# Moving the prompt attention's steps ahead in a hand-written issue order, and its first row loads to another queue

## The chip, the cores and the metric

The kernel runs on one core of a Trainium2 chip. The metric is the device time of one execution in microseconds (us), the median of several runs. The engines are TensorE (PE, with its weight loads as PEld), VectorE (DVE), ScalarE (ACT), GpSimd (POOL) and SyncE (SP). Each engine works through its own instructions strictly in the order that was fixed at compile time. Transfers are issued from the queues of SP (`dma` in the code), ACT (`put`) and POOL (`later`).

## What is computed

One layer of a hybrid decoder, in f32, for 512 prompt tokens and 8 sampled tokens that share all weights. They are handled together as 520 columns:

```
x = x + 0.5 * swiglu_1(rmsnorm(x))
z = rmsnorm(x) @ w_in          # u | q | k | v | gate_a | gate_b
a = gelu(ssm(u) + D*u);  a = a * sigmoid(a @ w_glu)         # branch A, state-space
b = mix over 3 groups of dilated window attention(q, k, v)  # branch B
x = x + (sigmoid(gate_a) * (a @ w_proj_a) + sigmoid(gate_b) * (b @ w_proj_b)) @ w_out
x = x + 0.5 * swiglu_2(rmsnorm(x))
```

Outputs are the new rows, the states of the state-space branch and the key and value caches.

## The kernel before

A *product* is 128 output rows times 520 columns. Each f32 operand is split into two fp32r parts (`wh`+`wl`, `xh`+`xl`), and the helper `mm` (line 221) adds three partial products over the blocks of the inner dimension, so a product over 1024 rows is 8 blocks x 3 x 2 column halves = 48 matmuls. The weights come in one at a time: `wfetch` loads a tile `wr` on SP's queue (L175), ACT copies it to `wh` (L166) and DVE forms `wl` (L167); three weights are kept ahead. There are 212 weights, and the products keep their order on PE.

Between the two SwiGLUs the products follow as: two q/k blocks, eight u blocks, ten q/k blocks, six v blocks, sixteen gate blocks, eight `w_glu` blocks (called glu0 to glu7 here, and gate0 to gate15 before them), then the projections. The smaller work of the branches is written as Python generators. Each has a list of numbers, and `pace()`, called after a product, counts the products and advances a generator once for each number that is reached. The count is 19 after gate0, 34 after gate15, 35 after glu0. In this order at each count:

- `LV`: `leave` (L765), the state-space output: 8 steps of 48 small matmuls (L772 to L774), copies by ACT, and after every second step eight stores to `yD` on POOL's queue (L787). Its last steps stand at 27, 27, 28, 28.
- `NB`: `normal` (L902): `normalise` of q/k block 0 to 11 by DVE (L863), each fed by two broadcasts on POOL's queue (L857), the last two at 20; then `tokens(0)` at 24.
- `AT`: the attention, 19 steps. Steps 1 to 16 are `attention(r)` for four row blocks `r`; two steps make a *pair* (one `r`, two heads for each of two halves `hp`): scores on PE (L960), bias and maxima on DVE (L966, L972), exponentials on ACT (L975), transposes on PE (L980) and their copies on ACT (L981), the sum over values on PE (L989) and its copy on ACT (L991). The pairs are numbered 0 to 7 here. Step 17 is `exchange` (four transfers), 18 and 19 are `combine`.
- `KS` and `SM`: the attention of the sampled tokens over the caches (`scores`, L1075, and `samples`, L1085), from 29 and from 34.
- `YB`: `y_block` 0 to 7 (L1050), from 29 to 33: two loads of a block from `yD` on POOL's queue (L1053, L1054), a gelu in turns on ACT and DVE (L1056 to L1060), and the split into `yh` (ACT, L304) and `yl` (DVE, L305). The tiles of the gelu have two buffers each, so block m+2 is loaded when block m is split. `yh` and `yl` lie in memory that the state-space tiles free when the last store of `leave` has landed.

The product glu0 multiplies all eight pairs `yh`, `yl`. Two planes of PSUM (tag `sb`) hold the scores of one pair, and two tiles `p` its exponentials.

The instructions other than the products stand on each engine where a planner put them at compile time: among those that are ready in its own reckoning of time, the one written first goes first. So a number in `AT` sets from which product on a step may be placed, and before which other work it goes.

At the start, `FIRST` (L38) orders the first transfers: numbers below 8 are the blocks of x (L370), 8 to 11 the halves of the first two weights (`whalf`, L187), 12 is the third weight. From each block of x ACT makes `xh` (L257) and a square (L269), DVE makes `xl` (L258).

Of the kernel before, what the change touches and what calls it, by code (L numbers as in the profile page):

```python
# [44 lines left out]
SC = 1.9  # L45
LV = (21, 21, 22, 22, 27, 27, 28, 28)
NB = (15, 15, 16, 16, 17, 17, 18, 18, 19, 19, 20, 20, 24)
AT = (25, 26, 27, 28, 29, 30, 31, 32, 32, 33, 34, 34, 35, 35, 36, 36, 37, 38, 40)
KS = (29, 30, 30, 31, 31, 32, 32, 33)
SM = (34, 34, 37, 39, 40)  # L50
YB = (29, 29, 30, 30, 31, 31, 32, 33)
# [7 lines left out]
def build(tc, A):  # L59
    nc = tc.nc  # L60
    V, S, G, T = nc.vector, nc.scalar, nc.gpsimd, nc.tensor
    dma = nc.sync.dma_start
    put = nc.scalar.dma_start
# [105 lines left out]
    def wfetch():  # L169
        ap = next(stream, None)  # L170
        if ap is None:
            return
        n = ap.shape[1]
        raw = raws.next()
        dma(raw[:, 0:n], ap)  # L175
        h, l = whs.next(), wls.next()
        wsplit(raw[:, 0:n], h[:, 0:n], l[:, 0:n])
        ahead.append([(h[:, c:c + 512], l[:, c:c + 512]) for c in range(0, n, 512)])


    def whalf(i, c):
        if c == 0:
            start.append((next(stream), raws.next(), whs.next(), wls.next()))
            ahead.append([])
        ap, *tiles_ = start[i]
        raw, h, l = (t[:, c:c + 512] for t in tiles_)
        dma(raw, ap[:, c:c + 512])  # L187
        wsplit(raw, h, l)
        ahead[i].append((h, l))
# [177 lines left out]
    X = [pf.tile([128, NT], F32, name="x", tag="x", bufs=KB) for m in range(KB)]  # L367
    for step in FIRST:
        if step < KB:
            dma(X[step], A["xT"][step])  # L370
        elif step < 12:
            whalf(step % 2, (step - 8) // 2 * 512)
        else:
            wfetch()
# [783 lines left out]
    def outputs():  # L1158
        while len(ys) < KB:
            y_block(len(ys))  # L1160
            yield

    side.append((list(AT), attending))
    yout = outputs()
# [78 lines left out]
    X = []  # L1243
# [123 lines left out]
```

## Time and profile before

| | |
|---|---|
| median of 3 runs | 1280.14 us (1277.73 to 1282.16) |
| time of the profiled execution | 1280.84 us |
| span from its first to its last instruction | 1279.0 us |
| PE, PEld busy | 98%, 96% of the span |
| DVE, ACT, POOL busy | 56%, 34%, 13% |
| mean granted TensorE clock | 0.992 of full speed |
| moved | 188.7 MB read, 68.6 MB written |

The shares are of one profiled execution. Matmuls are pipelined and the ends of their rows are modelled, so that the count of matmuls in a stretch and its length say more than the busy time. The clock is one of two levels, 1.2 GHz (0.5 of full speed) and 2.4 GHz. A row "A <- B" says that A sat idle until B released it.

### The profile page before, as it was taken

The numbers are of one execution on the slowest core, as the hardware profiler recorded it, in microseconds if no ns is written. First come the engines' busy times: TensorE is split into PE (matmuls) and PEld (weight loads), VectorE is DVE, ScalarE is ACT, GpSimd is POOL, SyncE is SP. The second block draws the span as 40 slices with busy tenths as digits, with TensorE's granted clock in tenths as the row PEclk, the third lists the DMA queues.
The fourth block names the chain that finished last, engine by engine and source line by source line (L and its number), as shares of the span: only waits on it lengthen the run. The fifth ranks groups of instructions, "written<-read, shape, count | busy, mean of one in ns | idle before, by whom it ended". The sixth has DMA issues, their size and how long they took to land.

```text
span 1279.0 us, 25230 instructions
## 1 busy us (share of the span) xinstructions
PE 1258.8 (98%) x10575; PEld 1234.1 (96%) x10575; DVE 714.8 (56%) x1268; ACT 434.7 (34%) x695; POOL 161.0 (13%) x289
## 2 busy tenths in 40 slices
PE   8999999999999999998999999999999999999999
PEld 7999999999999999998999789999999999999998
DVE  6794455635555339988436768765544334434442
ACT  5332233222344233342344664433423122222320
POOL 0110010000103541004631210000000000000000
PEclk9999999999999999999999889999999999999999
DMA  6665364637566575237957725547545445433332
GB/s 223 222 214 175 93 239 159 182 100 239 186 188 203 131 174 160 91 104 225 258 163 231 261 77 153 164 161 231 203 171 186 133 148 198 129 103 108 115 104 88
DMA packets 94889, 214.00 MB, mean 167 GB/s; under 512 B 42052, under 2 KB 50528, under 8 KB 94008
## 3 DMA queue, kind: packets, MB, share of 16 engines
q1 hardware_dynamic: 61640, 136.32, 34.1%
q0 software_dynamic: 13680, 67.62, 15.7%
q10 hardware_dynamic: 19456, 8.46, 2.7%
q8 instruction: 83, 1.36, 0.4%
q14 instruction: 30, 0.25, 0.1%
HBM read 188.72 MB, written 68.60 MB: 201 GB/s over the span
## 4 chain that ended last, share of the span: by engine, by line
PE 91%; DMA 4%; issue 1%; SPq 1%; POOL 1%; ACT 1%; DVE 0%; ACTq 0%; POOLq 0%; DVEq 0%
PE bigB L221 44%; PE bigA L221 29%; PE third L221 13%; PE s L681 1%; DMA kvt<-qkD 1%; PE s L989 1%; DMA ut<-uD 1%; PE sb L960 1%; DMA vD<-tok 1%; DMA gD<-t_sq 0%; PE s L980 0%; DMA x<-in_xT 0%; DMA wr<-in_wg 0%; PE bigB L774 0%; DMA OB<-hD 0%
## 5 line engine op out<-in xcount | busy, mean ns | idle before, releaser
L166 ACT ACTIVATE wh<-wr 128x1024 fp32r<-128x1024 f32 (+3 forms) x212 | 214.3, 1011 | 599.7 <-PE bigB L221 245.0
L167 DVE TENSOR_TENSOR wl<-wr,wh 128x1024 fp32r<-128x1024 f32 (+3 forms) x212 | 246.1, 1161 | 66.0 <-ACT wh L166 64.7
L221 PE MATMUL bigB<-xh,wh 128*128 128x260 f32 (+1 forms) x1216 | 249.1, 286 | 0.3 <-ACT wh L166 0.3
L221 PE MATMUL bigB<-xl,wh 128*128 128x260 f32 (+1 forms) x1216 | 248.7, 284 | 0.0
L221 PE MATMUL bigB<-xh,wl 128*128 128x260 f32 (+1 forms) x1216 | 246.9, 284 | 0.0
L221 PEld LDWEIGHTS bigB<-xl,wh 128*128 128x128 f32 x1216 | 188.1, 188 | 2.4 <-issue 2.4
L221 PEld LDWEIGHTS bigB<-xh,wh 128*128 128x128 f32 x1216 | 187.6, 189 | 1.6 <-issue 0.5
L221 PEld LDWEIGHTS bigB<-xh,wl 128*128 128x128 f32 x1216 | 187.9, 188 | 0.9 <-issue 0.9
L221 PE MATMUL bigA<-xh,wh 128*128 128x260 f32 x704 | 143.3, 285 | 2.4 <-ACT xh L257 1.5
L221 PE MATMUL bigA<-xl,wh 128*128 128x260 f32 x704 | 142.4, 284 | 0.7 <-DVE xl L258 0.7
L221 PE MATMUL bigA<-xh,wl 128*128 128x260 f32 x704 | 142.1, 283 | 0.5 <-DVE wl L167 0.5
L120 POOL COPY pace<-ah 1x1 f32<-1x1 f32 x48 | 21.6, 449 | 750.2 <-ACT ah L301 750.2
L221 PEld LDWEIGHTS bigA<-xh,wh 128*128 128x128 f32 x704 | 109.0, 190 | 4.7 <-ACT xh L257 3.3
L221 PEld LDWEIGHTS bigA<-xl,wh 128*128 128x128 f32 x704 | 108.6, 189 | 1.4 <-DVE xl L258 1.4
L221 PEld LDWEIGHTS bigA<-xh,wl 128*128 128x128 f32 x704 | 108.9, 189 | 0.7 <-DVE wl L167 0.7
L221 PE MATMUL bigA<-ah,wh 128*128 128x260 f32 x352 | 71.2, 283 | 0.0
L221 PE MATMUL bigA<-al,wh 128*128 128x260 f32 x352 | 71.0, 283 | 0.0
L221 PE MATMUL bigA<-ah,wl 128*128 128x260 f32 x352 | 70.6, 282 | 0.0
L221 PE MATMUL third<-xh,wh 128*128 128x260 f32 x288 | 58.0, 282 | 0.0
L221 PE MATMUL third<-xh,wl 128*128 128x260 f32 x288 | 57.9, 283 | 0.0
L221 PE MATMUL third<-xl,wh 128*128 128x260 f32 x288 | 57.8, 282 | 0.0
L221 PEld LDWEIGHTS bigA<-ah,wh 128*128 128x128 f32 x352 | 54.2, 189 | 0.1
(386 smaller groups left out, 2071.2 us busy)
## 6 DMA issues: line engine op xcount, KB each, us to landing
out_okv<-in_kv POOLq DMA_DIRECT2D x32, 1023.5 KB, 6.4
wr<-in_wg SPq DMA_DIRECT2D x43, 512.0 KB, 3.6
wr<-in_wu SPq DMA_DIRECT2D x43, 512.0 KB, 3.6
wr<-in_win SPq DMA_DIRECT2D x42, 512.0 KB, 4.3
wr<-in_wd SPq DMA_DIRECT2D x32, 448.0 KB, 3.4
wr<-in_wd SPq DMA_DIRECT2D x16, 512.0 KB, 3.4
out_okv<-in_kv POOLq DMA_DIRECT2D x8, 1022.0 KB, 5.9
kvt<-in_kv SPq DMA_DIRECT2D x48, 128.0 KB, 4.5
```

Source lines behind the costliest of these rows:

```text
L120: ins = G.tensor_copy(pace[0:1, 0:1], t[0:1, 0:1])
L166: S.activation(h, raw, AF.Copy)
L167: V.tensor_tensor(l, raw, h, ALU.subtract)
L221: i = T.matmul(ps[:, hf, 0:x.shape[1]], lhsT=a[:, c], rhs=x, start=k == 0 and j == 0, stop=k == n - 1 and j == 2)
L681: mark(T.matmul(ps[:, ri], lhsT=mp[:, a * 2 + ri], rhs=ut[:, a, 8:CW], start=True, stop=True))
L960: T.matmul(o, lhsT=q[pr, qc], rhs=k[pr, kc], start=True, stop=True)
L989: T.matmul(po[x * 64:x * 64 + 64, l * 128:l * 128 + 128], lhsT=vt[:, kt, c:c + 64], rhs=pTs[x][:, j], start=j in (j0, 2), stop=j % 2 == 1)
```

## The change

The numbers of `AT` become smaller, so that the attention's pairs are written after gate4 to gate11 (the last one in two halves, at 30 and 31) instead of after gate6 to glu1; `exchange` goes from 37 to 32, the two halves of `combine` from 38 and 40 to 33 and 36. The eight blocks of x are loaded from ACT's queue instead of SP's.

```diff
-AT = (25, 26, 27, 28, 29, 30, 31, 32, 32, 33, 34, 34, 35, 35, 36, 36, 37, 38, 40)
+AT = (23, 23, 24, 24, 25, 25, 26, 26, 27, 27, 28, 28, 29, 29, 30, 31, 32, 33, 36)
...
     for step in FIRST:
         if step < KB:
-            dma(X[step], A["xT"][step])
+            put(X[step], A["xT"][step])
         elif step < 12:
             whalf(step % 2, (step - 8) // 2 * 512)
```

No other line changes.

## Rows read from the trace of the kernel before

**Rows 1.** Windows, line 221 alone: length, busy (matmuls), clock, DMA share, GB/s.

```profile
792.45:895.81 103.36, 103.36 (x867) 103.36 (x866) 1.00 0.57 186
682.30:691.80 9.50, 7.31 (x49) 6.04 (x48) 1.00 0.87 275
717.93:748.46 30.53, 8.77 (x49) 7.49 (x49) 0.72 0.39 126
```

**Rows 2.** Windows, whole: PE, PEld, DVE, ACT, POOL busy, clock, DMA share, GB/s.

```profile
0.00:28.85 28.85, 24.36 (x157) 19.71 (x157) 18.96 (x44) 16.76 (x25) 2.14 (x10) 0.94 0.71 229
7.30:10.70 3.40, 3.35 (x15) 2.75 (x14) 2.35 (x5) 2.81 (x5) 0.00 (x0) 0.50 0.91 252
727.50:744.60 17.10, 14.84 (x84) 11.43 (x83) 11.62 (x23) 9.96 (x28) 3.67 (x6) 0.50 0.12 32
```

**Rows 3.** PE's groups of the stretch 717.93:748.46: count, busy us, mean ns, idle before.

```profile
L989 PE MATMUL s<-pT,vt 128*64 128x128 f32 x48 | 6.6, 375 | 0.2 <-ACT pT L981 0.2
L960 PE MATMUL sb<-qk 64*128 64x128 f32 (+1 forms) x26 | 5.4, 376 | 0.0
L980 PE MATMUL s<-ident,p 128*128 128x128 f32 x24 | 4.8, 343 | 1.2 <-ACT p L975 1.2
```

**Rows 4.** Timeline of ACT and DVE: first and last split of the y blocks.

```profile
683.67 0.63 ACT L304 ACTIVATE yh<-t_G 128x520 fp32r<-128x520 f32 x1
...
745.66 0.68 DVE L305 SCALAR_TENSOR_TENSOR yl<-t_G,yh 128x520 fp32r<-128x520 f32 x1
```

**Rows 5.** Groups of 640:748.5, ACT's of the attention, DVE's of y.

```profile
L975 ACT ACTIVATE p<-p,own 128x256 f32<-128x256 f32 (+1 forms) x30 | 14.6, 488 | 7.1 <-DVE own L972 7.0
L981 ACT ACTIVATE pT<-s 128x512 f32<-128x512 f32 (+1 forms) x16 | 8.9, 568 | 13.1 <-PE s L980 8.6 <-DMA kvt<-qkD 4.6
...
L1060 DVE SCALAR_TENSOR_TENSOR t_G<-t_T,t_G 128x520 f32<-128x520 f32 x8 | 5.5, 693 | 0.3 <-ACT t_T L1059 0.2
```

**Rows 6.** Timeline: the last normalised block (DVE), pair 0's last scores (PE).

```profile
630.53 0.75 DVE L863 SCALAR_TENSOR_TENSOR qk<-OB,gains,qk 128x512 f32<-128x512 f32 x1
...
634.17 0.49 PE L960 MATMUL sb<-qk 64*128 64x128 f32 x4
```

**Rows 7.** Timeline of POOL: last stores of `leave`; loads of y blocks 3, 5, 7.

```profile
670.16 4.23 POOL L787 DMA_DIRECT2D yD<-XS  x8 [8.44 <-ACT XS L780]
...
686.76 0.75 POOL L1053 DMA_DIRECT2D t_G<-yD  x1
...
714.16 0.76 POOL L1053 DMA_DIRECT2D t_G<-yD  x1 [2.73 <-DVE yl L305]
...
730.38 0.75 POOL L1053 DMA_DIRECT2D t_G<-yD  x1 [0.42 <-DVE yl L305]
```

**Rows 8.** Tile `t_G`, 684:748: its loads, from issue to landing.

```profile
DMA to landing us min/median/max: 3.0/5.1/6.3
```

**Rows 9.** Timeline of ACT, 698:706: a store that ACT issues, and what follows it.

```profile
704.13 0.33 ACTq L887 DMA_DIRECT2D gD<-t_sq  x1
704.51 0.60 ACT L981 ACTIVATE pT<-s 128x512 f32<-128x512 f32 x1 [4.56 <-DMA kvt<-qkD]
```

**Rows 10.** Timeline of the start: ACT's first work, SP's third weight, PE's waits.

```profile
0.74 1.28 ACT L166 ACT_TABLE_LOAD   x1 [0.74 <-PEq L1359]
3.85 0.63 ACT L166 ACTIVATE wh<-wr 128x512 fp32r<-128x512 f32 x1 [1.82 <-DMA wr<-in_wg]
...
5.78 0.50 PE L221 MATMUL bigA<-xh,wh 128*128 128x260 f32 x2 [1.48 <-ACT xh L257]
...
14.56 0.33 SPq L175 DMA_DIRECT2D wr<-in_wg  x1
...
21.67 0.51 PE L221 MATMUL bigA<-xh,wh 128*128 128x260 f32 x2 [0.84 <-ACT wh L166]
...
22.93 0.50 PE L221 MATMUL bigA<-xh,wl 128*128 128x260 f32 x2 [0.52 <-DVE wl L167]
```

**Rows 11.** SP's waits in 0:40: who waited for whom, us, times, longest.

```profile
SPq L397 <- DMA x<-in_xT: 0.3, 1, 0.3
```

## The prediction

> **What bounds the kernel now.** First the page: PE is busy for 98% of the span, so only time in which PE waits, or runs at the lower clock, can be won. Then the windows, to find where that time lies. In the stretch after 792 us PE does nothing but products: 867 matmuls in 103.36 us, 0.119 us each, 5.72 us for a product [rows 1]. Two stretches are worse. The first three products need 144 x 0.119 = 17.2 us and are done only at 28.85 us, where the first stretch of [rows 2] ends. And glu0 takes 30.53 us for 49 matmuls, that is 24.7 us more than they cost [rows 1]. Third, the groups of PE inside glu0: the scores of some two pairs, the transposes of three and the value sums of three [rows 3], so the attention's last pairs are done inside this product. Last, the timeline of the y blocks: glu0 multiplies them, the last one is split at 745.66 + 0.68 = 746.34 us [rows 4], and glu0 ends 2.1 us later, at 748.46. So in this stage the chain of y blocks ends last, not PE's work; the attention only fills the wait. While PE filled it with small matmuls, its granted clock went to the lower level, 0.50 from 727.5 to 744.6 us [rows 2].
>
> **The cost of a pair.** Gate12 held one whole pair: 9.50 us with 49 product matmuls [rows 1], which cost 5.84; the pair's 36 small matmuls and the switches cost 3.7 us. On ACT the 30 exponentials and 16 copies of 640 to 748.5 us took 14.6 + 8.9 us [rows 5], about 3 us a pair; on DVE a pair has two instructions each of L966 and L972, with 512 columns like L1060's 0.69 us: 2.7 us.
>
> **The numbers 23 and 24.** Pair 1 needs q/k block 11. It was normalised at 630.53 us, in gate6, and pair 0's last scores ran at 634.17, just behind gate6 [rows 6], which is where 25 puts them. So the two products of advance can be used by pair 0 only in part; pair 1 can go about two products earlier (behind gate6 and not behind gate8), and from there on one pair fits a product. Pairs 4 to 7, now between gate13 and glu1, come to stand at about gate10 to gate13. ACT and DVE have room: a product with a pair is 9.5 us long, and the pair takes 3 and 2.7 of them. I take no new wait of PE there; if that cover fails, a place costs what a late ACT cost PE once in the start, 0.84 us (below). Bounds 0 and, with four such places, +3.4 us.
>
> **What leaves glu0.** Some 2.7 pairs x 3.7 = 10 us of PE work go to earlier products and cost the same there: nothing is won by that itself. What can be won is the rest, 14.7 us, less what the sampled tokens' small matmuls take in it, which stay (no row here prices them; I leave 2, between 0 and 4): 12.7 us, of which the lower clock is up to 14.84 / 2 = 7.4 [rows 2]. It is won only if the y blocks come earlier.
>
> **The y chain.** Here the edit pulls both ways.
> - Later start. `yh` waits for the last store of `leave`, issued from 670.16 us on for 4.23 us [rows 7]. `leave`'s last steps stand behind gate8 and gate9, and with the new numbers pairs 2 and 3 go before or between them. PE is full there, so the chain starts 2 x 3.7 = 7.5 us later. Bounds: 3.7 (one pair) and 9.
> - Shorter chain. Loads of block 3, 5 and 7 were issued at 686.76, 714.16 and 730.38 us [rows 7]: the turns took 27.4, 16.2 and 16.0 us (the last to 746.34). One block alone needs 0.75 of issue, 5.1 to land [rows 8], and six instructions at 0.4 to 0.7 on ACT and DVE, 4.4 us, so 10.3 us. A turn with two blocks in step has some 2 us more, 12.3. The difference, 15 us in the first turn and 3.8 in each later one, is time behind other work in the two queues. The first turn keeps as many pairs as before. In the second and third no pair is left, but the sampled tokens are. I take 3.5 us from each of these and 4 us from the first, whose worst piece is a 4.56 us stop of ACT [rows 9] that need not come again in that place: 11 us. Bounds 4 and 17.
>
> So the last split moves by 7.5 - 11 = -3.5 us, to 742.8. To this come the value sums of pair 7, which stood in glu1: a third of the 6.6 us of [rows 3], halved for the full clock, 1.1 us. And of the 2.1 us between the last split and glu0's end, the last block's 12 matmuls need 1.4; the other 0.6 was small matmuls that move too. Against it: PE then has nothing left in its last wait, and I count one 3.4 us stretch at half speed, as at 7.3 to 10.7 us [rows 2], that now falls on product work: +1.7. The row shows the fall behind a stretch of small, broken work. The Trainium skill's "TensorE: Matmul & The Clock Gate", section "What's actually happening", says that the throttled state is the default and that activity releases it; this trace agrees, with 0.50 at 727.5 to 744.6 us. By that rule an emptier glu0 is no cure for the clock. Sum of this part: -3.5 - 1.1 - 0.6 + 1.7 = -3.5 us.
>
> **The loads of x.** The first products start at 5.78 us [rows 10] and lose 28.85 - 5.78 - 17.2 = 5.9 us. SP gets rid of eight issues. The third weight's load, now issued at 14.56 us, can go earlier; its lateness cost PE 0.84 + 0.52 = 1.4 us. But ACT must now issue them: at 0.33 us each, as for its store [rows 9], 2.6 us. ACT had 1.82 us free before its first copy at 3.85 us and a table load of 1.28 before that [rows 10]; where that load now stands behind the issues, and the issues fill more than the free time, the first copy is 1 us late. And an issue can wait. SP's load of `lim` waited for a block of x [rows 11], with which it shares nothing; counted back, that block was the eighth transfer before it. ACT's store at 704.13 us did the same: ACT stood for 4.56 us until a `kvt` load had landed [rows 9]. With 13 transfers at the start, some of ACT's eight will wait that way, in front of its first copy if they stand there. So: bounds -3.4 (the 1.4, and the lower clock's 3.4 / 2 and 0.3 of small waits) and +3 us (the first copy behind the landing of the fourth block); I take -0.5. Against a gain speaks "DMA: Bandwidth & Descriptors", section "Issuing engines are not separate DMA queues", of the Trainium skill: transfers from all engines run on the same 16 engines, and a second issuer saves only the time of issuing. The trace has a DMA share of 0.71 in this stretch [rows 2], so it leaves some room. By the rule alone this part would be 0 and the sum 0.5 us higher.
>
> **Sum.** -3.5 - 0.5 = -4.0 us. On the profiled execution, 1280.84 us, that is 1276.8; it lies 0.7 above the median of 1280.14, so I expect 1276.
>
> **Rivals.**
> - *PE alone is the bound* (the chain shortens by 17 us and more): gates end at 717.9 + 10 = 728, glu0 adds 5.7 + 2, nothing is lost: -12.7 and the start's -0.5, 1267. For it: the turns were twice as long as one block needs. Against: the later start, and two turns of landing times that no edit shortens.
> - *The gain is eaten*: the pairs in front of `leave` cost the chain as much as it wins behind it, and the time stays within 2 us, 1279.5. For it: the 7.5 us are sure as long as PE is full there, the 11 are an estimate.
> - *Slower, by ACT's issues*: if the planner puts all eight in front of the first copy, the fifth to eighth wait for landings of x blocks, as [rows 11] shows it for `lim`, and ACT makes its first copy at 8 us instead of 3.85. It decides from a first copy after 6 us on. PE's losses there absorb a part of the 4 us; +3 at the start and a chain that wins nothing give 1283. Against it: the planner may put the first copy ahead of the later issues.
>
> **How the numbers follow.** About 0.3% (3.8 us) is what a measurement of this kernel can tell from no change. Chances: the forecast (-8 to -1, 1272 to 1279) 0.46, PE alone 0.12, eaten 0.24, slower 0.18. Of the forecast 0.30 lie beyond 0.3%, 0.16 within; eaten is 0.22 within and 0.02 slower; the slower rival gives 0.16 slower and 0.02 within. So faster 0.42, same 0.40, slower 0.18. The range of 1267 to 1283.5 reaches from PE alone to the slower rival.
>
> **What would show it.** In the profile after: pair 7's scores before gate14 and no L960 inside glu0; `leave`'s last stores some 7 us later than 670; turns of the y loads of 12 to 13 us at the end; glu0's start at about 727 and its end near 745; still a half-clock stretch about there. At the start, ACT's first copy near 4.5 us, the third weight's load before 14 us. The prediction is wrong if the pairs do not come forward (the planner holds them for block 11), if the first y turn grows because four pairs share it, or if ACT's first copy comes after 6 us.

## The result

The changed kernel is slower: 1288.20 us in the median of 5 runs (1286.90 to 1291.06) against 1280.14, a ratio of 1.007 with a 95% interval of 1.0051 to 1.009. Forecast were 1276 us, and a range of 1267 to 1283.5. The profiled execution took 1288.08 us, its span is 1286.3, 7.3 more than before.

### The profile page after: what moved, and what is told of

It reads as the page before. It is cut to its first block, busy times and chain, and to the rows that moved or that the text cites. A ratio compares the mean times of both kernels' runs of the same rounds, so it can differ in the third digit from the quotient of the medians.

```text
span 1286.3 us, 25230 instructions
## 1 busy us (share of the span) xinstructions
PE 1260.1 (98%) x10575; PEld 1234.1 (96%) x10575; DVE 715.3 (56%) x1268; ACT 432.7 (34%) x693; POOL 159.3 (12%) x289
## 4 chain that ended last, share of the span: by engine, by line
PE 92%; DMA 3%; DVE 2%; issue 1%; ACT 1%; SPq 0%; ACTq 0%; POOL 0%; DVEq 0%
PE bigB L221 44%; PE bigA L221 30%; PE third L221 13%; PE s L681 1%; PE sb L960 1%; DMA wr<-in_win 1%; DMA x<-in_xT 1%; DVE wl L167 1%; PE bigB L772 1%; DMA kvt<-in_kv 1%; PE bigB L773 1%; PE bigB L774 1%; PE s L989 1%; DMA kvt<-qkD 0%; DMA wr<-in_wglu 0%
```

## The profile after

The stretch of pure products costs what it did [rows 1], and glu0 is 6 us shorter than before. Windows of line 221 alone: length, busy (matmuls), clock, DMA share, GB/s.

```profile
799.67:903.03 103.36, 103.36 (x866) 103.36 (x865) 1.00 0.57 186
732.89:757.45 24.56, 9.01 (x51) 7.34 (x49) 0.72 0.77 228
```

The 7.3 us are found by laying the starts of the products of both traces side by side. The fourth product starts at 32.42 instead of 28.85 us: +3.6. From there to gate0 the changed kernel wins 1.5, from gate0 to gate4 1.0. From gate4 to gate10 it loses 16.4 (69.5 us instead of 53.1). From gate10 to glu0 it wins back 2.6, in glu0 6.0, in glu1 to glu7 1.8. So 16.4 us of PE time went in front, 10.4 us came off behind, and of the start's loss 1.1 us were left at gate4. The 16.4 us are no spread between executions: gate4 to gate10 takes 53.06 to 53.09 us in the five kernels with the old order there (before, e2, e4, e5 and e9 below) and 69.46 to 69.50 in four with the new one (the change, e1, e7 and e12).

What went in front are small matmuls of the attention, without a wait of PE. Windows from the start of gate4 to that of gate10, line 960 (scores) alone in the changed kernel, in the one before, and in gate12 of before; then line 980 (transposes) alone in the changed kernel and in the one before:

```profile
617.83:687.33 69.50, 10.64 (x64) 7.67 (x64) 1.00 0.53 160
616.75:669.81 53.06, 2.61 (x20) 1.64 (x20) 1.00 0.72 208
682.30:691.80 9.50, 1.02 (x12) 0.91 (x12) 1.00 0.87 275
617.83:687.33 69.50, 6.60 (x36) 4.21 (x36) 1.00 0.53 160
616.75:669.81 53.06, 2.45 (x12) 1.52 (x12) 1.00 0.72 208
```

With the value sums (line 989: 72 and 24, shown below) these are 44 + 24 + 48 = 116 small matmuls more. A pair has 36, so they are 3.2 pairs, and each costs 5.1 us of the 16.4. The scores are the dear part: 44 more take 8.0 us.

What left glu0 are the pairs: no row of L960, L980 or L989 is in it [rows 3]. What is left are the sampled tokens, and waits: PE is idle for 9.0 us of it, before for 3.4. PE's groups of 732.89 to 757.45 us:

```profile
L1137 PE MATMUL sb<-kvt,pk 128*32 128x256 f32 x38 | 5.9, 568 | 0.8 <-DMA kvt<-in_kv 0.4 <-DVE pk L1122 0.3
L221 PE MATMUL bigB<-yh,wh 128*128 128x260 f32 x17 | 4.5, 347 | 2.9 <-ACT yh L304 2.9
...
L1121 PE MATMUL s<-ident,L 32*128 32x32 f32 x3 | 0.5, 295 | 4.6 <-DVE L L1117 4.6
```

The y chain, in the timelines of POOL and DVE; the rows answer to [rows 7] and to the last split of [rows 4]:

```profile
686.62 4.18 POOL L787 DMA_DIRECT2D yD<-XS  x8 [17.07 <-ACT XS L780]
700.11 0.75 POOL L1053 DMA_DIRECT2D t_G<-yD  x1
727.55 0.75 POOL L1053 DMA_DIRECT2D t_G<-yD  x1 [0.96 <-DVE yl L305]
742.14 0.78 POOL L1053 DMA_DIRECT2D t_G<-yD  x1
755.34 0.69 DVE L305 SCALAR_TENSOR_TENSOR yl<-t_G,yh 128x520 fp32r<-128x520 f32 x1
```

`leave`'s last stores come 16.5 us later than before, the last split ends at 756.03, 9.7 us later, so between the two the chain won 6.8. The turns are 27.4, 14.6 and 13.9 us (before 27.4, 16.2 and 16.0): the first has not become shorter at all.

The windows of the start and of the two stretches at the lower clock (columns as in [rows 2]) and, below, ACT's first work with one row each of PE and SP (the timeline; they answer to [rows 10]):

```profile
0.00:32.42 32.42, 23.82 (x156) 20.50 (x157) 21.08 (x62) 17.19 (x27) 2.14 (x10) 0.84 0.67 213
7.07:17.30 10.23, 5.48 (x23) 5.19 (x24) 6.49 (x14) 7.41 (x13) 0.00 (x0) 0.50 0.89 301
740.93:754.58 13.65, 8.42 (x43) 4.72 (x43) 9.78 (x18) 4.89 (x10) 5.67 (x11) 0.50 0.69 168
```

```profile
0.74 1.86 ACTq L370 DMA_DIRECT2D x<-in_xT  x4
2.63 1.28 ACT L166 ACT_TABLE_LOAD   x1 [2.63 <-issue]
5.44 0.63 ACT L166 ACTIVATE wh<-wr 128x512 fp32r<-128x512 f32 x1 [1.53 <-DMA wr<-in_wg]
5.45 1.02 ACTq L370 DMA_DIRECT2D x<-in_xT  x2
7.86 0.63 ACT L166 ACTIVATE wh<-wr 128x512 fp32r<-128x512 f32 x1 [1.79 <-DMA wr<-in_wu]
8.65 1.82 ACTq L370 DMA_DIRECT2D x<-in_xT  x2
10.52 0.63 ACT L166 ACTIVATE wh<-wr 128x512 fp32r<-128x512 f32 x1 [2.03 <-DMA x<-in_xT]
11.06 0.71 ACT L257 ACTIVATE xh<-x,wn 128x520 fp32r<-128x520 f32 x1
11.82 0.80 PE L221 MATMUL bigA<-xh,wh 128*128 128x260 f32 x2 [7.64 <-ACT xh L257]
13.24 0.36 SPq L175 DMA_DIRECT2D wr<-in_wg  x1
```

The eight issues are spread over ACT's first ten microseconds, and all of them, with three copies of weights, stand in front of the first `xh`. The last group of two takes 1.82 us because an issue in it waits; by the profile the copy behind it was released by a block of x, with which it shares nothing. PE starts at 11.82 instead of 5.78 us, and its clock stays at half speed until 17.3 us, before until 10.7 [rows 2].

## The experiments

In each comparison the kernel before ran beside the others; its medians were 1279.1 to 1279.5 us. Single runs of it lay between 1272.9 and 1286.8, so a difference of a few us between two profiled executions proves little by itself. "From SP" below means that the loads of x are issued as before. The columns: start of `leave`'s last eight stores, end of the last split of y (both in the profiled execution), median time, and ratio to before with its interval.

| kernel | stores | split | us | ratio |
|---|---|---|---|---|
| before | 670.2 | 746.3 | 1280.1 | |
| the change | 686.6 | 756.0 | 1288.2 | 1.0070 (1.0051 to 1.0090) |
| e1 steps only | 682.9 | 753.9 | 1285.6 | 1.0052 (1.0033 to 1.0070) |
| e2 x only | 672.6 | 742.6 | 1282.0 | 1.0019 (1.0003 to 1.0036) |
| e3 pairs 2 to 7 behind leave | 670.5 | 744.0 | 1280.2 | 1.0010 (0.9990 to 1.0030) |
| e4 x, four by ACT | 665.7 | 736.6 | 1280.1 | 0.9999 (0.9979 to 1.0018) |
| e5 before, sampled later | 670.9 | 741.7 | 1279.6 | 1.0004 (0.9989 to 1.0018) |
| e6 all pairs behind | 664.1 | 736.8 | 1288.6 | 1.0077 (1.0053 to 1.0101) |
| e7 steps, sampled later | 685.2 | 753.4 | 1287.6 | 1.0063 (1.0045 to 1.0081) |
| e8 as e6, sampled later | 665.9 | 741.6 | 1279.2 | 1.0003 (0.9985 to 1.0021) |
| e9 x behind first copies | 669.7 | 743.2 | 1278.5 | 0.9991 (0.9974 to 1.0007) |
| e10 pairs 2 and 3 in front | 678.7 | 748.4 | 1280.8 | 1.0017 (1.0004 to 1.0030) |
| e11 leave earlier | 663.1 | 738.0 | 1283.7 | 1.0036 (1.0020 to 1.0052) |
| e12 steps, combination back | 682.0 | 750.2 | 1283.4 | 1.0037 (1.0020 to 1.0053) |
| e13 steps, gate stores by POOL | 683.7 | 749.9 | 1285.0 | 1.0043 (1.0025 to 1.0061) |
| e14 before, gate stores by POOL | 674.3 | 742.5 | 1280.0 | 1.0009 (0.9993 to 1.0026) |
| e15 as e14, x four by ACT | 678.9 | 745.6 | 1284.4 | 1.0044 (1.0028 to 1.0060) |

### The two parts alone

e1 keeps the new `AT` and loads x from SP; e2 keeps the old `AT` and loads x from ACT.

> Only the numbers of AT are changed; the blocks of x are loaded from SP's queue as before. Theory: of the 7.3 us that the span grew, the attention's steps cost the greater part, because the pairs now stand on PE in front of the last steps of leave, and the y blocks, which glu0 waits for, start that much later. Expected: the first product at about 5.8 us, the last stores of leave issued at about 684 (before 670, after 686.6), the end of glu0 about 754 (before 748.5, after 757.5), time 1283 to 1286 us. Rival: the late start of PE after the loads by ACT does the harm, and the steps alone cost nothing: 1279 to 1281.5 us.

> Only the loads of x are issued by ACT; the numbers of AT are those of before. Theory: ACT's later issues of x wait in front of its first xh, so PE's first product starts at about 11.8 us and not at 5.8, and of these 6 us some 3.6 are left at the fourth product (38.2 against 34.6); the rest of the trace moves with it. Expected: time 1282 to 1284.5 us. Rival: the start's loss is made up later, where PE waits anyway for the chain of y blocks: within 1.5 us of before.

Both theories hold, that of e2 narrowly (its interval begins at 1.0003): 1.0052 and 1.0019, and 0.52% + 0.19% is the 0.7% of the whole. In e1 the first product starts where it did before, the last stores at 682.9 and glu0 ends at 755.4. In e2 PE starts at 11.0 us and the fourth product at 31.5; the time lies just under the range that was expected.

### The start: four issues, or the same eight in another place

e4, with the old `AT`:

```diff
-            put(X[step], A["xT"][step])
+            (put if step < 4 else dma)(X[step], A["xT"][step])
```

> AT as before; only the first four blocks of x are loaded by ACT, the other four by SP. Theory: it is the wait of ACT's fifth and later issues for earlier transfers, in front of the first xh, that makes PE late, and not the issuing as such. Expected: ACT issues four loads without a wait, its first copy comes about 1 to 1.5 us later than 3.85, PE's first product at 6 to 7.5 us, the third weight's load earlier than 14.56, time 1278.5 to 1281 us. Rival: the loads themselves (ACT's time for issues, the table load behind them, the transfers that come all at once) delay the first xh: first product at 9 us or later, time 1282 us or more.

e9, with the old `AT`; the first four blocks are issued as in the change:

```diff
-        if step < KB:
+        if step < 4:
             put(X[step], A["xT"][step])
+        elif step < KB:
+            pass
...
     for m in range(KB):
+        if m == 3:
+            for i in range(4, KB):
+                put(X[i], A["xT"][i])
         n1.add(X[m])
```

> AT as before; all eight blocks of x are still issued by ACT, but the last four are written behind the work on the first three blocks, so that the first xh stands in front of them on ACT. Theory: not the number of ACT's issues but their place, in front of the first xh, makes PE start at 11 us. Expected: first xh before 7 us, PE's first product at 6.5 to 7.5 us, the fourth product no later than 30 us (31.5 with all eight in front), time 1279 to 1281 us. Rival: issues that wait on ACT hold up the copies wherever they stand: PE starts early but waits as long behind its first blocks, the fourth product starts at 31 us or later, time 1282 us.

Timeline of PE, the first row of e2, of e4 and of e9:

```profile
11.00 0.80 PE L221 MATMUL bigA<-xh,wh 128*128 128x260 f32 x2 [6.42 <-ACT xh L257]
```

```profile
6.63 0.50 PE L221 MATMUL bigA<-xh,wh 128*128 128x260 f32 x2 [2.05 <-ACT xh L257]
```

```profile
6.51 0.80 PE L221 MATMUL bigA<-xh,wh 128*128 128x260 f32 x2 [1.93 <-ACT xh L257]
```

Four issues in front of the first copy cost no time, and eight by ACT cost none either when the last four stand behind the first `xh` (one of them still stops ACT, for 0.84 us). So it is their place. The fourth product starts at 27.4 us in e4 and at 27.9 in e9, against 28.85 before. That is no gain that can be told: the twelve kernels here that load x from SP start it between 26.91 (e13) and 28.85 us (before), and no gain can be seen in the medians either.

### The steps: what stands in front of `leave`

All with x from SP. e3 holds pairs 2 to 7 behind `leave`'s numbers 27 and 28, e10 only pairs 4 to 7; e6 puts all eight pairs behind.

```diff
 # e3
+AT = (23, 23, 24, 24, 29, 29, 29, 29, 30, 30, 30, 30, 31, 31, 31, 31, 32, 33, 36)
 # e10
+AT = (23, 23, 24, 24, 25, 25, 26, 26, 29, 29, 29, 29, 30, 30, 30, 30, 32, 33, 36)
 # e6
+AT = (29, 29, 30, 30, 31, 31, 32, 32, 33, 33, 34, 34, 35, 35, 36, 36, 37, 38, 40)
```

> x loaded from SP's queue; AT of the change, but pairs 2 to 7 are held until 29, behind the last steps of leave, and then four steps to a product; exchange and combine at the numbers of the change. Theory: what delays the end is the pairs' PE work in front of leave's last steps. Expected: leave's last stores at 673 to 677, the end of glu0 some 6 to 9 us earlier than with the steps alone, time 1277 to 1281 us. Rival: the turns of the y blocks are set by the sampled tokens' scores and loads on DVE and the DMA engines, however early leave ends: the last stores come early, the last split of y does not, and the time stays within 2 us of that of the steps alone.

> x by SP; pairs 2 and 3 at the numbers of the change, in front of leave's last steps, pairs 4 to 7 held until 29, behind them. It lies between the steps of the change (1285.6) and those with all of pairs 2 to 7 behind (1280.2). Theory, that each pair in front costs the chain its own PE time of 3.7 us less what the later work gives back: leave's last stores at 679 to 683, time 1281.5 to 1284.5 us. Rival: the loss comes from the dense pairs at the change's later numbers (four pairs within one y turn), not from the place of leave: within 1.5 us of either neighbour.

> x by SP; AT so that all eight pairs stand behind leave's last steps (two steps to a product from 29 to 36), exchange and combine as before: the steps moved the other way. Theory: every pair in front of leave's last steps delays the y chain by about 3.7 us. Without pairs 0 and 1 there, leave's last stores come about 7 us earlier than before (666 to 668), the last split of y at 738 to 744, time 1274 to 1279 us. Rival: the pairs then take ACT and DVE in the turns of the y blocks, which grow by as much: the last split stays at 746 or later, time 1279 us or more.

How many pairs stood in front of the end of `leave` is counted by their value sums, 12 rows each for pairs 0 and 1 and 16 for each later one. Windows of line 989 alone from the start of gate0 to that of gate10, in the kernel before, in the changed one, in e3 and in e10:

```profile
574.99:669.81 94.82, 2.53 (x24) 1.64 (x24) 1.00 0.74 219
```

```profile
577.09:687.33 110.24, 7.17 (x72) 4.75 (x72) 1.00 0.63 189
```

```profile
572.16:669.18 97.02, 2.60 (x24) 1.64 (x24) 0.98 0.75 215
```

```profile
573.20:677.36 104.16, 5.65 (x56) 3.71 (x56) 0.98 0.68 199
```

Two pairs before, five in the changed kernel, two in e3, four in e10. e3 has nearly all of the change's edits, its pairs denser still, and is 5.5 us faster than e1. Two things differ in its order: pairs 2 to 5 stand behind `leave`, and since the pairs end later, the combination stands behind the last split (from 757.3 us on; in e1 three pieces of it stand in front). e12 below moves the combination back and leaves the pairs where they are, and still loses 0.37% to before. So the place of pairs 2 to 5 in front of `leave` costs; how the 5.5 us divide between the two is less sure. The price in time is not linear. e10's stores are as late as expected, 8.2 us behind e3's, yet its time is 0.6 us longer only. So its time fell where the rival put it, but the rival's cause is not it: e3 has the dense pairs too, all of them in the y turns, and loses nothing. Its last split comes 4.4 us later than in e3, but in e3 glu1 to glu3 take 20.8 us, with small matmuls in them, and in e10 17.3. I read this as a wait in glu0 that work from behind fills, for the first two pairs; no run tests that by itself. e1, with one pair more and the next one's scores in front, and with three pieces of the combination ahead of the last split where e10 has one, takes 4.8 us more than e10.

e6 answers a second question. Its last stores are 6 us earlier than before, its last split 9.6, and it is as slow as the change. Not all of the 6 and 9.6 us is the edit's: gate4 to gate10 is 3.5 us shorter (49.5 us), but the rest may be the spread between executions, since e4, with the old `AT`, has its last split at 736.6 too. Timeline of PE: some of pair 0's scores in the kernel before and in e6; window whole of glu1 and glu2 in e6, and of the same two products in e8:

```profile
612.29 0.71 PE L960 MATMUL sb<-qk 64*128 64x128 f32 x8
```

```profile
645.03 0.49 PE L960 MATMUL sb<-qk 64*128 64x128 f32 x4
```

```profile
737.40:762.02 24.62, 21.04 (x160) 17.50 (x158) 11.96 (x17) 16.89 (x26) 3.68 (x6) 0.86 0.29 78
```

```profile
742.39:756.13 13.74, 13.74 (x119) 13.06 (x118) 8.85 (x18) 8.57 (x13) 2.08 (x4) 1.00 0.28 82
```

First, pair 0 has the number 29, reached after gate10 at 669.3 us, and stands at 645.0. The description of the kernel above has it that a number sets from which product on a step may be placed. The number does not hold a step back; it only says which of two ready steps goes first. The trace of before had shown it: pair 0's number is 25, reached after gate6, and its first eight scores stand in gate3. Second, with the pairs late, pairs and sampled tokens meet in glu1 and glu2. Of the 24.6 us PE is idle for 3.6 and at half speed for 6.8, and 61 small matmuls start there, in e8 21.

e11 pulls `leave` itself forward, with the old `AT`:

```diff
-SC = 1.9
-LV = (21, 21, 22, 22, 27, 27, 28, 28)
+SC = 2.1
+LV = (19, 19, 20, 20, 25, 25, 26, 26)
```

> x by SP and AT as before; the scan that leave needs is spread over fewer products (SC 2.1 for 1.9) and leave's eight steps are written two products earlier (LV 19, 19, 20, 20, 25, 25, 26, 26). The hinge of the theory pulled the other way, with no pair moved: leave's last stores come 8 to 12 us earlier than 670, the last split of y 5 to 10 us earlier than 746, and glu0 waits less: time 1273 to 1277 us. Rival: what the y blocks win is lost again, since the pairs that went before leave now stand in glu0 or PE waits for the scan: within 2 us of before or slower.

The rival holds: stores 7 us and last split 8 us earlier, time 1.0036. glu1 and glu2 take 23.3 us here as well (the profiled execution is the slowest of its twelve). I read it so: an early y chain is worth something only as long as it is the last to end.

### The sampled tokens

e5 is the kernel before, e7 is e1, e8 is e6, each with

```diff
-KS = (29, 30, 30, 31, 31, 32, 32, 33)
-SM = (34, 34, 37, 39, 40)
+KS = (32, 32, 33, 33, 34, 34, 35, 35)
+SM = (36, 36, 38, 40, 41)
```

> The kernel before (its AT, x by SP) with the sampled tokens' steps alone moved: KS from 29-33 to 32-35, SM from 34-40 to 36-41. Theory: what makes the first turn of the y blocks 27 us long, in the kernel before as after the change, is the sampled tokens' scores (eight pairs of instructions of 0.96 and 0.95 us on DVE, and the cache loads they wait for) in front of the gelu on DVE. Expected: the first turn 15 to 19 us, the last split of y 5 to 9 us earlier than 746, time 1272 to 1277 us. Rival: the wait only changes its place, PE then waits in glu1 to glu4 for the sampled tokens' softmax and its small matmuls run there at the lower clock: within 2 us of before.

> The steps alone (x by SP) with the sampled tokens' steps moved as well: KS 32-35, SM 36-41. Theory of two parts: the pairs in front of leave delay the chain's start, and that part stays (last stores about 686); the sampled tokens lengthen the first turn, and that part goes (27 us to under 20), with PE's wait of 5.3 us for the sampled softmax inside glu0. Expected: time 1277 to 1281 us. Rival: with the start late, the turns are bound by their own transfers and the sampled tokens don't matter: 1284 us or more.

> All eight pairs behind leave and the sampled tokens later (x by SP). If both parts of the theory hold, the y blocks come early and glu0 waits for nothing: leave's last stores at 666 to 668, the last split at or before 735, time 1268 to 1274 us. Rival: the work that is moved behind fills ACT and DVE up to the projections, and the branch b is late for them: 1279 us or more.

The edit did not do what it was meant for. The sampled tokens' scores still begin in the first turn in e5, at 687.7 us, and in e7 the softmax hardly moved: its last step on DVE stands at 744.62, in e1 at 745.06. So whether those scores lengthen the first turn was not tested by it. What e5 moved is the softmax, out of glu0, and that is worth nothing (1.0004). e8 shows when it is worth much: behind e6's late pairs it takes 9.5 us away, and gives the kernel's old time, not the 1268 to 1274 us that were expected.

### Inside the turns

e12 is e1 with the exchange and the combination put back; e13, e14 and e15 issue the stores of the gate blocks from POOL.

```diff
 # e12
+AT = (23, 23, 24, 24, 25, 25, 26, 26, 27, 27, 28, 28, 29, 29, 30, 31, 37, 38, 40)
 # e13 (on e1), e14 (on before), e15 (on e4)
-        put(gD[i], t)
+        later(gD[i], t)
```

> The steps alone (x by SP) with the exchange and the combination put back to 37, 38 and 40. Theory: with the steps of the change, the combination's products and sums on DVE (1.22 and 1.12 us, twice) stand in front of the last split of y, 3 to 4 us of the chain's end. Expected: last split of y 3 to 4 us earlier than with the steps alone (753.9), time 1282 to 1283.5 us. Rival: the combination is hidden, the place of the pairs alone decides: 1284.5 to 1286.5 us.

Timeline of DVE at the end of the chain, in e1 and in e12:

```profile
748.71 1.22 DVE L1032 TENSOR_TENSOR OB<-OB,vt 128x1024 f32<-128x1024 f32 x1
750.45 1.11 DVE L1033 TENSOR_TENSOR ob<-OB 128x512 f32<-128x512 f32 x1
752.08 1.23 DVE L1032 TENSOR_TENSOR OB<-OB,vt 128x1024 f32<-128x1024 f32 x1
753.21 0.71 DVE L305 SCALAR_TENSOR_TENSOR yl<-t_G,yh 128x520 fp32r<-128x520 f32 x1
```

```profile
749.52 0.68 DVE L305 SCALAR_TENSOR_TENSOR yl<-t_G,yh 128x520 fp32r<-128x520 f32 x1
750.81 1.23 DVE L1032 TENSOR_TENSOR OB<-OB,vt 128x1024 f32<-128x1024 f32 x1 [0.61 <-DMA vt<-wD]
```

In e1, as in the changed kernel, three pieces of the combination (1.22 + 1.11 + 1.23 us) stand in front of the last split; in e12 they stand behind it, the split comes 3.7 us earlier, and the median is 2.2 us lower, as expected; the two intervals overlap, so the size of this is not sure.

> The steps alone (x by SP) with the stores of the gate blocks issued from POOL's queue and not ACT's. Theory: in the first turn of the y blocks ACT stands 3.4 us at such a store, which waits for a cache load, and the second block's gelu waits behind it. Expected: no such stop on ACT, the first turn 25 us and not 27, time 1282 to 1284.5 us. Rival: the first turn is set by DVE (the sampled tokens' scores): time within 1.5 us of 1285.6.

> The kernel before with the stores of the gate blocks issued from POOL's queue. Theory as for the steps alone: ACT's stop of 4.56 us goes, the first turn of the y blocks is 2 to 4 us shorter, time 1275.5 to 1278 us. Rival: the stop is hidden behind DVE's work, or the stores delay the y loads on POOL's queue: 1278.5 us or more.

> The kernel before with the gate stores on POOL's queue and the first four blocks of x loaded by ACT, whose fourth product started 1.4 us earlier than before. If both win: 1274 to 1277 us. Rival: as for the gate stores alone: 1278 us or more.

The stop of ACT is real in the changed kernel. Timeline of ACT in its first turn:

```profile
708.64 0.33 ACTq L887 DMA_DIRECT2D gD<-t_sq  x1
709.29 0.39 ACT L991 ACTIVATE OB<-s 128x256 f32<-128x256 f32 x1 [3.41 <-DMA kvt<-in_kv]
```

Without it the first turn is 24.9 us instead of 27.7 in e13, and 20.8 instead of 27.4 in e14, and the last splits come 4 us earlier. The medians don't follow, and neither theory holds: 0.6 us below e1, and 1.0009 of before. (e13's profiled execution is 4.1 us below e1's, as the shorter turn would give, but it is the fastest of its twelve runs.) For e14 the trace shows why. The edit did more than it was meant to: the planner now puts 48 more small matmuls of the attention in front of gate10. Window whole of gate4 to gate9 in e14:

```profile
611.91:672.96 61.05, 59.66 (x493) 55.99 (x491) 21.57 (x37) 27.57 (x71) 28.29 (x50) 1.00 0.61 185
```

This is 8.0 us more than before, and the first turn gave 6.6. So e14 does not price the stop alone; e13, whose gates hold as many matmuls as e1's, does, and what it is worth in time stays open. e15 is slower than e14 by 4.3 us although e4 alone cost nothing. Its gates take as long as e14's (60.9 us), and its fourth product does not start early (28.1 us), so the two gains that it was to add were not there; I have no shown cause for the loss. No version here beats the kernel before by more than its measurement can tell.

## Why the prediction was wrong, point by point

- **What leaves glu0** was right: the pairs are gone from it, pair 7's scores stand before gate14, and glu1 to glu7 win 1.8 us, where 1.1 was counted for pair 7's value sums.
- **Later start of the y chain** is the step that failed: "pairs 2 and 3 go before or between them ... so the chain starts 2 x 3.7 = 7.5 us later", with a bound of 9. The chain starts 16.5 us later, 14.4 of it after gate0. Both factors were too small. Not two pairs came in front but three whole ones and the scores of the next, 3.2 pairs by their small matmuls. And a pair cost 5.1 us there, not 3.7; e10 gives the same (70 small matmuls more than before, 10.0 us). The price had come from gate12 alone, where twelve scores took 1.02 us, 0.085 each; in front of gate10 each of the 44 more took 0.18. Why scores cost double there, no run shows. The count was wrong because I took the numbers of `AT` as places where the pairs come to stand. They are ranks, as e6 and the early scores of before show: a pair that outranks `leave`'s last steps, or ties with them at 27 and 28 and is ready while they wait, goes in.
- **Shorter chain**, 11 us with bounds of 4 and 17: 3.7 us from the load of block 3 to the last split, and 3.1 between the last stores and that load, which the prediction did not count. So the last split moved by 16.5 - 6.8 = +9.7 us and not by -3.5. The later turns gave 1.6 and 2.1 where 3.5 each was taken, though the combination came into the last one; I had given it no price, and with it put back e12's split comes 3.7 us earlier and its median 2.2. The first turn gave nothing. Its "worst piece", the "4.56 us stop of ACT ... that need not come again in that place", came again with 3.4 us. And seven of the eight scores of the sampled tokens fall into that turn on DVE again, since their loads start later too (at 696.8 us, before at 679.6). Groups of DVE from 700.11 to 727.55 us:

```profile
L1080 DVE TENSOR_TENSOR kvt<-kvt 128x768 f32<-128x768 f32 x7 | 6.7, 952 | 5.9 <-DMA kvt<-qkD 5.9
L1081 DVE TENSOR_REDUCE sc<-kvt 128x12 f32<-128x768 f32 x7 | 6.6, 945 | 0.0
```

  That these 13.3 us and the wait set the turn's length is argued from the rows; no run took them away.
- **The clock.** One stretch at half speed of 3.4 us was counted, at +1.7. It lasts 13.65 us, 740.93 to 754.58, but PE is busy in 8.42 of them only, so it costs at most 4.2; before, 17.1 us with 14.84 busy [rows 2]. It begins behind waits of 2.3 and 0.7 us for `yh` and `yl`. At the start, where the clock was a possible gain, the stretch grew from 3.4 to 10.2 us (5.48 busy). "By that rule an emptier glu0 is no cure for the clock": the rule of the Trainium skill ("TensorE: Matmul & The Clock Gate", section "What's actually happening") is that the lower level is the default and activity lifts it. The trace agrees as far as it goes: glu0's mean clock is 0.72 before and after. In the stretch of before, which the prediction took as agreeing with the rule, PE was busy for 87%; what made the clock fall there is not shown.
- **No new wait in the gates** was right. The new wait is in glu0: 4.6 us for the sampled tokens' softmax (2.0 before). It ends before the last split does. e5 took the shorter wait out of the kernel before and won nothing; out of the changed kernel no run took it.
- **The loads of x.** -0.5 was taken, +2.4 measured (e2's and before's medians give 2.9). The mechanism was that of the rival: issues that wait, in front of ACT's first work. But its mark was badly chosen. ACT's first copy came at 5.44 us, before the 6 that were to decide, and was a copy of a weight; what PE waits for is the first `xh`, at 11.06. The third weight's load did come earlier, 13.24 for 14.56, and PE does not wait between 17.3 and 32.42 us; that its 1.4 us shorten the start is not shown, as e4's fourth product lies within the spread. What the Trainium skill says in "DMA: Bandwidth & Descriptors", section "Issuing engines are not separate DMA queues", that a second issuer saves issuing time at best, agrees with e4 (0.9999) and e9 (0.9991): no gain in the time.
- **The rivals.** The slower one had the start right (+3 there) and the chain "that wins nothing". What none of them had is a chain that ends later than before because its start moves by more than the work that is taken out of its turns.

## What to carry to other kernels

Before steps are moved forward in an order that a planner fills, count what PE work then outranks the step that the last chain starts from, from the ranks and from what is ready, and not from the places that the numbers seem to name. Price it from more than one place: a pair took 3.7 us in one gate and 5.1 in others. Where the engine was full, all of it delayed that chain; behind it, only what filled a wait came back. And ask of a load that is moved to a working engine's queue which instruction of that engine is needed first, and keep the issues that may wait behind it.

## What was not expected of the hardware

- An issue by ACT that must wait stops ACT's arithmetic behind it: 2.03 us at 10.52 us of the start, and 3.41 us in the first turn, both ended, by the profile, by a transfer with which the next instruction shares nothing.
- The stretch at half clock moves and shrinks with the order of the work: 17.1 us before, 13.65 after, 3.4 in e5. The products glu1 and glu2 ran at 1.00 in e8 and at 0.86 in the mean in e6, whose PE waited in them for 3.6 us.
- The kernel before spreads over 1272.9 to 1286.8 us, so that one profiled execution may lie some us from the median: e13's took 1281.49 us, its median is 1285.01.
